# An earlier table of cache products, the first attention block inside the last projection chunk, and a split order for the output projection

## The chip, the cores and the metric

The kernel runs on one core of a Trainium2 chip. The metric is device time in microseconds (us) for one launch. The engines are named as in the profile: PE (matrix multiplies and transposes), PEld (its weight loads), DVE (vector), ACT (scalar, activations), POOL (GpSimd), SP (here it only issues DMAs). Every engine works through its own instructions strictly in the order of its program and waits on semaphores of the others.

## The reference

One inference step of a two-layer trunk for 512 prompt tokens and 8 x 8 sample tokens, all in float32. Layer 0 mixes by dilated attention, layer 1 by a diagonal state-space layer; each is followed by a gated feed-forward layer. The change touches layer 0's attention alone:

```python
DIL_GROUPS = ((128, 1), (512, 4), (2048, 16)); HEAD_DIM = 64; N_HEAD_SLOTS = 8
qkv = (h @ w_qkv).reshape(B, T, 3, N_DIL, N_HEAD_SLOTS, HEAD_DIM)
q = rope(rmsnorm(qkv[:, :, 0], q_gain), pos)
k = rope(rmsnorm(qkv[:, :, 1], k_gain), pos)
v = qkv[:, :, 2]
...      # per group: keys = cache + new, scores * 64**-0.5, keys at 0, d, 2d, ..., window
p = jnp.exp(s - lse[..., None])
o = jnp.einsum('bqhk,bqkhd->bqhd', p, vf)
wts = jax.nn.softmax(jnp.stack(lses, axis=0), axis=0)
return jnp.einsum('gbqh,gbqhd->bqhd', wts, jnp.stack(outs, axis=0)) @ w_o
```

The prompt has no cache. Each of the 8 sample rows (b = 0..7, 8 tokens each) attends to its own cache of 128, 512 and 2048 positions; a query uses 129 keys of each group.

## The kernel before

**The projection** (`qkv_phase`) makes q, k and v for three groups in nine chunks of 512 columns, in the order of `CHUNKS`. A chunk has four steps, so there are 36 steps, j = 0..35. A step takes 256 rows of `w_qkv`: each weight tile is split into a rounded high part `whi` (ACT) and a remainder `wlo` (DVE), and PE multiplies four tiles of 128 prompt tokens (`xh`, `xl`) and one of the sample tokens (`xsp`) into five PSUM tiles `acc`. At a chunk's end ACT and DVE evict the five tiles (`a`); for q and k DVE then does norm and rotation over the next steps (`finish`: three instructions for each tile, table `TURNS`), and PE transposes the results. v of group 1 is the last chunk.

**Cache work woven into the steps.** After each `acc` tile of a step comes a slot (`slot`), in which PE gets a little of other work, five slots to a step. Three kinds of it bear on this case:

- *Units of keys* (`SCORES`, class `Score`): for a sample row b and group 1 or 0, PE transposes cached keys (`pt<-ident,kc`), ACT evicts them (`ks<-pt`), and PE multiplies them with the row's queries into a PSUM tile `Sd` (`Sd<-ks,Q..`). DVE then masks `Sd` into `Sall` and takes a maximum (`Sall<-Sd,md`, `mx`).
- *Pairs* (`PAIRS`): for group 2, SP loads a tile of cached keys and the row's queries from DRAM (`kc<-cache_kv_w`, `kc<-qscr`, 512 KB each), and DVE multiplies them and sums over a head (`kc<-kc`, `P<-kc`). The pairs of step j are loaded in step j-1 and queued on DVE at the start of step j, behind the step's `wlo` and `finish` work. A row has four pairs.
- *Close* (`Close2`): ten slots after a row's fourth pair was queued, or later if a unit is half done, PE transposes the row's sums into `Sd` (`Sd<-ident,P`, `Sd<-kT,Q`), and DVE masks them like a unit's.

There is one `Sd` buffer: the next user's matmuls wait until DVE has read the last one's. The orders of PE, DVE, ACT and SP here are kept as written (`kept`, `keep_in_program_order`).

**Attention** (`attn_phase`) runs 16 blocks n (four head pairs by four token residues): score matmuls `S` (`scores`), mask and maximum on DVE (`masked`: `sm<-S,mp`), exponential on ACT (`exps`), transposes of the probabilities (`turn`: `pt<-ident,sm`), and products with v (`values`: `O`). Beside them the eight sample rows are worked (`Decode`): softmax of the row's scores `Sall` (maximum `dnm`, exponential, reciprocal, scale), transposes into `Sd`, products with cached values (`Sd<-kc,Pz`, 27 MB of values come in by SP), the row's own v (`vn`, by way of DRAM, `vscr`), and the copy into `att`.

**The output projection** (`wo_phase`) splits `att` into `ath` (ACT) and `atl` (DVE), splits four weight tiles of `w_o` as above, and multiplies.

Of the kernel before, what the change touches and what calls it, by code (L numbers as in the profile page):

```python
# [18 lines left out]
D = 1024  # L19
# [4 lines left out]
KT = 8  # L24
# [27 lines left out]
def _build(nc, tc, A, es):  # L52
# [71 lines left out]
    with ExitStack() as qs:  # L124
        atp = right("atp")
        at_ = atp.__enter__()
        att = at_.tile([128, 4, NT], F32, name="att")
        rs_ = ExitStack()
        dsp = rs_.enter_context(right("dsp"))
        Sall = dsp.tile([128, NB, 3, 136], F32, name="Sall")  # L130
        mx3 = dsp.tile([128, NB, 3], F32, name="mx3")
        md = dsp.tile([128, 3, 136], BF16, name="md")
        kst = rs_.enter_context(right("kst", bufs=KST))
        qk = qs.enter_context(pool("qk"))
        qT = [att] + [qk.tile([128, 4, NT], F32, name=f"qT{i}") for i in (1, 2)]
        kT = [qk.tile([128, 4, NT], F32, name=f"kT{i}") for i in range(3)]
        vscr = scr.tile([3, 64, 512], F32, name="vscr")
        qscr = scr.tile([64, 512], F32, name="qscr")
        vtscr = scr.tile([4, 128, 512], F32, name="vtscr")
        xscr = scr.tile([128, KT, NT], F32, name="x_scr")  # L140
        with ExitStack() as p1:
            acc = p1.enter_context(tc.tile_pool(name="acc", bufs=5, space=PSUM))
            c1 = p1.enter_context(pool("c1"))
            vt, mp = qkv_phase(nc, tc, A, p1, locals())
        with ExitStack() as p2:
            attn_phase(nc, tc, A, p2, locals())
        rs_.close()
# [184 lines left out]

def qkv_chunk(nc, L, x, begin, step, pre=None, slot=None):
    acc = L["acc"]
# [6 lines left out]
    for kk in range(4):  # L341
        wh, wl = begin()
        for t in range(4):
            if pre is not None:
                pre(kk, t)
            for k2 in range(2):
                k = kk * 2 + k2
                ah, al = x.h[:, k, t * 128:(t + 1) * 128], x.l[:, k, t * 128:(t + 1) * 128]
# [5 lines left out]
        for k2 in range(2):  # L354
            k = kk * 2 + k2
            mm(ps[4], x.s[:, k, :], wh[:, k2, :], start=k == 0, stop=False)
            mm(ps[4], x.s[:, k, :], wl[:, k2, :], start=False, stop=k == KT - 1)
        if slot is not None:
            slot()
        step()  # L360
# [54 lines left out]
def qkv_phase(nc, tc, A, es, L):  # L415
# [77 lines left out]
    def begin():  # L493
# [6 lines left out]
        for gi in SCORES.get(j, ()):  # L500
            b, n = fill[gi].pop(0), UNITS[gi]
            cached.append((gi, b, [cache_tile(nc, A, kst, "kc", gi, b, c0, min(2, n - c0), 0, kept) for c0 in range(0, n, 2)]))
        due = [ready.pop(0) for _ in range(PAIRS.get(j, 0))]
# [138 lines left out]

    def v_chunk(gi, wk, vt=None):
        ps = qkv_chunk(nc, L, x, begin, step, None, slot)
        for t in range(5):
            if t == 4:
# [8 lines left out]
            kv_out(nc, A, gi, 1, t, a)  # L655

    for part, gi in CHUNKS[:8]:
# [10 lines left out]

    def values():
        nc.sync.dma_start(vt0, L["vtscr"].rearrange("t p c -> p t c"))  # L670
        nc.sync.dma_start(mp, A["c_mp"])

    notes[34] = values
# [5 lines left out]
    return [vt0, vt1, vt2], mp  # L679

# [10 lines left out]
def attn_phase(nc, tc, A, es, L):  # L691
# [19 lines left out]

    den, rd, S2, PT, sm, P0, P12, O = {}, {}, {}, {}, {}, {}, {}, {}

    def scores(n):
# [3 lines left out]
        S2[n] = [pS.tile([128, 512], F32, name="S") for _ in range(2)]  # L718
        for b in range(4):
            for h in range(2):  # L720
                o, k = S2[n][h][b * 32:b * 32 + 32, 0:256], kT[0][half[h], hp, max(b - 1, 0) * 128:(b + 1) * 128]
                if not b:
                    o, k = o.rearrange("p (a c) -> p a c", a=2), k[:, None, :].to_broadcast([64, 2, 128])
                mm(o, qT[0][half[h], hp, r * 128 + b * 32:r * 128 + b * 32 + 32], k, start=True, stop=True, tile_position=(h * 64, b * 32))
        sl = slice(r * 128, r * 128 + 128)
        for gi in (1, 2):
            for h in range(2):
                mm(S2[n][h][:, (gi + 1) * 128:(gi + 2) * 128], qT[gi][half[h], hp, sl], kT[gi][half[h], hp, sl], start=True, stop=True)

# [6 lines left out]
    def exps(n, h):  # L736
        x, nm = sm[n][h]
        s.activation(x, x, AF.Exp, bias=nm, scale=-1.0, accum_out=den[n // 4][:, n % 4, h:h + 1])

# [21 lines left out]

    def values(n):
        hp, r = divmod(n, 4)
# [9 lines left out]
        for b in range(4):  # L773
            for pv in (1, 0):
                if b == 0 and pv == 0:
                    continue
                for j in range(4):
                    mm(o_[j * 32:j * 32 + 32, :, b, :], vt[0][:, b - 1 + pv, hp * 128 + j * 32:hp * 128 + j * 32 + 32], P0[hp][j // 2][:, pv, b],
                       start=False, stop=True, tile_position=(0, j * 32))
        R = pS.tile([128, 512], F32, name="S")  # L780
        for c in range(4):
# [9 lines left out]
    class Decode:  # L791
        def __init__(self, b):
            self.b, self.u = b, 0
            P = Sall[:, b].rearrange("p a b -> p (a b)")
            nm, dn, rd = (dk.tile([128, 1], F32, name=x, bufs=2) for x in ("dnm", "ddn", "drd"))
            v.tensor_reduce(nm, mx3[:, b, :], AX.X, OP.max)
            v.tensor_scalar(nm, nm, -SCALE, None, op0=OP.mult)
            s.activation(P, P, AF.Exp, bias=nm, scale=SCALE, accum_out=dn)
            v.reciprocal(rd, dn)
            v.tensor_scalar(P, P, rd, None, op0=OP.mult)  # L800
            self.pw = dk.tile([128, 24], F32, name="pw")
            v.tensor_copy(self.pw.rearrange("p (a b) -> p a b", a=3), Sall[:, b, :, 128:136])
            self.vn = dk.tile([24, 512], F32, name="vn", bufs=2)
# [46 lines left out]

    dec = {}
    for n in range(20):
        if n < 16:
            scores(n)
        if 1 <= n < 17:
            turn(n - 1)
        if n < 16:
            masked(n)
        for h in range(2):
            if 1 <= n < 17:  # L860
                evict(n - 1, h)
            if n < 16:
                exps(n, h)
        if n % 2 and n // 2 < 8:
            dec[n // 2].turn()
        if n % 2 == 0 and 0 <= n // 2 - 2 < 8:
            dec[n // 2 - 2].out()
        if 2 <= n < 18:
            values(n - 2)
            dec[n // 2 - 1].values(n % 2)  # L870
        if n % 2 == 0 and n < 16:
            dec[n // 2] = Decode(n // 2)


def wo_phase(nc, tc, A, es, L):
    v, s, g, te = nc.vector, nc.scalar, nc.gpsimd, nc.tensor
    pool, xT, att, load_w, mm6, acc, n0 = (L[x] for x in ("pool", "xT", "att", "load_w", "mm6", "acc", "n0"))
# [4 lines left out]
    atl = wk.tile([128, 4, NT], F32R, name="atl")  # L882
    for k in range(4):
        s.activation(ath[:, k], att[:, k], AF.Copy)
        v.tensor_tensor(atl[:, k], att[:, k], ath[:, k].bitcast(F32), OP.subtract)
    for c in range(4):
        wh, wl = load_w(A["w_o"], D, 0, 4, c * 256, 256, 0.0)
        for m in range(2):
            ps = acc()
            for k in range(4):  # L890
                mm6(ps, wh[:, k, m * 128:(m + 1) * 128], wl[:, k, m * 128:(m + 1) * 128], ath[:, k], atl[:, k], k == 0, k == 3)
            f = 2 * c + m
            xv = xr[:, f, :T].rearrange("p (r i) -> p i r", r=4)
            for h, i0, i1 in ((0, 0, 72), (1, 72, 128)):
                v.tensor_tensor(xT[:, f, 4 * i0:4 * i1].rearrange("p (i r) -> p i r", r=4), ps[:, h, :4 * (i1 - i0)].rearrange("p (i r) -> p i r", r=4), xv[:, i0:i1], OP.add)
            v.tensor_tensor(xT[:, f, T:], ps[:, 1, T - HN:HN], xr[:, f, T:], OP.add)
            n0.add(2 * c + m)
# [598 lines left out]
```

## Time and profile before

| | us |
|---|---|
| three runs | 1518.72, 1525.94, 1526.87 (median 1525.94) |
| the profiled execution | 1525.21 |
| its span | 1523.4 |
| PE busy | 1480.0 (97%) |
| projection, to the first `S` matmul | 0 to 319.5 |
| attention, to the first matmul with `ath` | 319.5 to 419.5 |

Spans and starts are in us from the start of the span. A row of the timeline gives start, duration, engine, line, operation, output<-input, shapes, the count, and in brackets how long the engine had been idle before it and what ended that. A row of the waits gives who waited for whom, the total, the number of times and the longest. PEclk in a row by windows is the granted PE clock, 1.00 being full speed.

### The profile page before, as it was taken

The page shows a single profiled execution, that of the slowest core. Times are in us where ns is not written, and L with a number is a line of the kernel's source. Part 1 is how long each engine was busy: PE and PEld are TensorE (multiplying, and loading weights), DVE is VectorE, ACT ScalarE, POOL GpSimd, SP SyncE. Part 2 cuts the span into 40 slices and gives each one's busy share as a digit, 9 for nine tenths or more (in the row PEclk, how much of TensorE's full clock was granted, in tenths as well). Part 3 has the DMA queues.
Part 4 walks back from the last instruction along what each step waited for, and adds up shares of the span by engine and source line. Part 5 has one row for each costly group of instructions (what it writes and reads, how often), then busy time and mean ns, then how long its engine had stood idle before and what let it go on. Part 6 is the DMA issues. An engine that isn't in the chain of part 4 may idle for free. (4 is left out here: it accounts for less than half of the span.)

```text
span 1523.4 us, 29540 instructions
## 1 busy us (share of the span) xinstructions
PE 1480.0 (97%) x12406; PEld 1388.4 (91%) x12406; DVE 910.8 (60%) x1507; ACT 520.9 (34%) x790; POOL 315.2 (21%) x369
## 2 busy tenths in 40 slices
PE   9999999789999999999999999999999999999998
PEld 7877777557799999999999999899999999999998
DVE  5899988545467853688887568754443333333332
ACT  4523445345553221222123363432332212221222
POOL 2021132310031019544434330020110001000100
PEclk9999999979999999999999999999999999999999
DMA  7568587979775555797666828865546555442222
GB/s 253 190 242 299 187 288 236 345 261 311 256 231 191 194 199 195 243 302 257 240 242 238 301 97 252 267 206 191 190 164 221 190 191 192 149 151 89 83 63 76
DMA packets 190460, 322.62 MB, mean 212 GB/s; under 512 B 39480, under 2 KB 137016, under 8 KB 188792
## 3 DMA queue, kind: packets, MB, share of 16 engines
q1 hardware_dynamic: 182808, 303.63, 58.3%
q10 hardware_dynamic: 4992, 10.04, 1.9%
q0 software_dynamic: 2528, 7.08, 1.3%
q8 instruction: 97, 1.59, 0.4%
q14 instruction: 35, 0.29, 0.1%
HBM read 289.22 MB, written 118.78 MB: 268 GB/s over the span
## 5 line engine op out<-in xcount | busy, mean ns | idle before, releaser
L107 PE MATMUL acc<-xgl,whi 128*128 128x288 f32 x1760 | 378.6, 296 | 1.0 <-DVE xgl L172 1.0
L107 PE MATMUL acc<-xgh,wlo 128*128 128x288 f32 x1760 | 377.7, 296 | 0.0
L107 PE MATMUL acc<-xgh,whi 128*128 128x288 f32 x1760 | 377.1, 296 | 0.1
L101 DVE TENSOR_TENSOR wlo<-raw,whi 128x1024 fp32r<-128x1024 f32 (+1 forms) x168 | 207.6, 1236 | 238.1 <-ACT whi L100 234.8
L100 ACT ACTIVATE whi<-raw 128x1024 fp32r<-128x1024 f32 (+1 forms) x168 | 174.5, 1039 | 458.6 <-PE acc L107 404.8
L107 PEld LDWEIGHTS acc<-xgl,whi 128*128 128x128 f32 x1760 | 282.6, 188 | 2.5 <-DVE xgl L172 1.3
L107 PEld LDWEIGHTS acc<-xgh,wlo 128*128 128x128 f32 x1760 | 282.7, 188 | 0.6 <-issue 0.2
L107 PEld LDWEIGHTS acc<-xgh,whi 128*128 128x128 f32 x1760 | 281.8, 188 | 0.5 <-DVE gt L933 0.3
L935 POOL TENSOR_TENSOR gt<-gt,rstd 128x576 f32<-128x576 f32 x44 | 77.1, 1754 | 431.1 <-ACT gt L934 431.0
L107 PE MATMUL acc<-hh,whi 128*128 128x288 f32 x704 | 151.4, 296 | 0.0
L107 PE MATMUL acc<-hh,wlo 128*128 128x288 f32 x704 | 151.2, 295 | 0.0
L107 PE MATMUL acc<-hl,whi 128*128 128x288 f32 x704 | 151.0, 295 | 0.0
L337 PE MATMUL acc<-whi,xh 128*128 128x512 f32 x288 | 119.7, 417 | 1.2 <-ACT a L688 0.7
L107 PEld LDWEIGHTS acc<-hh,wlo 128*128 128x128 f32 x704 | 113.2, 188 | 0.2 <-issue 0.2
L107 PEld LDWEIGHTS acc<-hl,whi 128*128 128x128 f32 x704 | 113.0, 188 | 0.2 <-issue 0.2
L337 PE MATMUL acc<-wlo,xh 128*128 128x512 f32 x288 | 113.1, 394 | 0.0
L107 PEld LDWEIGHTS acc<-hh,whi 128*128 128x128 f32 x704 | 113.1, 188 | 0.0
L337 PE MATMUL acc<-whi,xl 128*128 128x512 f32 x288 | 112.3, 395 | 0.0
L192 POOL TENSOR_TENSOR ssum<-ssum,sq 128x576 f32<-128x576 f32 x21 | 36.2, 1723 | 232.4 <-ACT sq L191 232.4
L337 PEld LDWEIGHTS acc<-whi,xh 128*128 128x128 f32 x288 | 54.6, 190 | 12.3 <-ACT a L688 1.7
L337 PEld LDWEIGHTS acc<-whi,xl 128*128 128x128 f32 x288 | 54.6, 190 | 12.1
L947 DVE TENSOR_TENSOR xT<-acc,xT 128x576 f32<-128x576 f32 x48 | 36.2, 754 | 48.1 <-PE acc L107 48.1
(362 smaller groups left out, 2015.9 us busy)
## 6 DMA issues: line engine op xcount, KB each, us to landing
o_kv_s<-cache_kv_w SPq DMA_DIRECT2D x64, 1020.0 KB, 7.5
kc<-cache_kv_w SPq DMA_DIRECT2D x96, 512.0 KB, 6.7
raw<-ffn_w_gate SPq DMA_DIRECT2D x44, 512.0 KB, 3.6
raw<-ffn_w_up SPq DMA_DIRECT2D x44, 512.0 KB, 3.6
raw<-ffn_w_down SPq DMA_DIRECT2D x40, 512.0 KB, 3.4
raw<-w_qkv SPq DMA_DIRECT2D x36, 512.0 KB, 6.5
kc<-qscr SPq DMA_DIRECT2D x32, 512.0 KB, 6.1
o_kv_s<-cache_kv_w SPq DMA_DIRECT2D x16, 1008.0 KB, 6.1
```

The lines of the kernel that those rows point to most:

```text
L100: s.activation(hi, raw, AF.Copy)
L101: mark[0] = v.tensor_tensor(lo, raw, hi.bitcast(F32), OP.subtract)
L107: te.matmul(ps[:, c, :HN], w, x[:, c * HN:(c + 1) * HN], start=first and i == 0, stop=last and i == 2)
L192: g.tensor_tensor(self.ss, self.ss, sq, OP.add)
L337: ins = nc.tensor.matmul(*a, **kw)
L935: g.tensor_tensor(t, t, nin.r, OP.mult)
L947: v.tensor_tensor(xv, ps[m][:, :, :HN], xv, OP.add)
```

## The change

1. `PAIRS`: one pair more in step 20 and in step 24, one fewer in steps 33 and 34. So rows 3 to 6 get their fourth pair 1 to 2 steps earlier, and their Close with it.
2. `SCORES`: group 1 has no unit in step 24, and its last six move on by one step (25 to 30); the eight units of group 0 come two at a time in steps 31 to 34, loaded by one 512 KB DMA into one buffer (before, two of 256 KB in two).
3. The last chunk (steps 32 to 35) works each step in the order samples, tiles 0 to 3, and in step 35 evicts each tile as it ends. Behind the sample tile, row 0's softmax is queued (`row_soft`); behind tile 0, the scores of attention block 0 (`score_block`, into the two `pt` buffers, with the masked result in two key buffers); behind tile 2, their exponentials. The attention loop starts with block 1.
4. At the end, row 7's last products come ahead of block 15's, and its output between block 15's products and its scaling.
5. `wo_phase`: the splits of the first two `w_o` tiles are queued behind the exponentials of block 6 (before: ACT 300.45 and 318.63 in the profile), and for the first of them all products with `ath` come ahead of those with `atl`. Two `ffn_w_gate` loads and a cache shift, `o_kv_s` (2 MB together), which SP issued from 303 on, move into the middle of the attention.
6. The loads of the mask `mp` and of `vt0` keep their place on SP in steps 34 and 35 (before, both in 34).

```diff
-PAIRS = {..., 19: 1, 21: 1, 22: 1, 23: 1, 24: 1, 25: 1, ..., 31: 1, 32: 2, 33: 2, 34: 2}
-SCORES = {22: (1,), 23: (1,), 24: (1,), ..., 29: (1,), 30: (0,), 31: (0, 0), 32: (0, 0), 33: (0, 0), 34: (0,)}
+PAIRS = {..., 19: 1, 20: 1, 21: 1, 22: 1, 23: 1, 24: 2, 25: 1, ..., 31: 1, 32: 2, 33: 1, 34: 1}
+SCORES = {22: (1,), 23: (1,), 25: (1,), ..., 30: (1,), 31: (0,), 32: (0,), 33: (0,), 34: (0,)}
...
+    notes[34] = lambda: kept(nc.sync.dma_start(mp, A["c_mp"]))
+    notes[35] = lambda: kept(nc.sync.dma_start(vt0, L["vtscr"].rearrange("t p c -> p t c")))
+    def then(t):
+        if t == 4:
+            row_soft(v, s, Sall, mx3, 0, *soft)
+        if t == 0:
+            S0.extend(ptp.tile([128, 4, 128], F32, name="pt").rearrange("p a b -> p (a b)") for _ in range(2))
+            score_block(lambda *a, **kw: kept(te.matmul(*a, skip_group_check=True, **kw)), S0, qT, kT, 0)
+            sm0.extend((kst.tile([128, 2, 512], F32, name="kc")[:, 0, :], f) for f in (f0, f1))
+            for h in range(2):
+                v.tensor_tensor_reduce(sm0[h][0], S0[h], mp[:, 0, :], -SCALE, 3e38, OP.add, OP.min, sm0[h][1])
+        if t == 2:
+            for h in range(2):
+                s.activation(sm0[h][0], sm0[h][0], AF.Exp, bias=sm0[h][1], scale=-1.0, accum_out=den0[:, 0, h:h + 1])
     with ExitStack() as e4:
-        v_chunk(1, e4.enter_context(pool("wk2")), vt1)
+        v_chunk(1, e4.enter_context(pool("wk2")), vt1, (4, 0, 1, 2, 3), then)
...
+def row_soft(v, s, Sall, mx3, b, nm, dn, rd, pw):
+    P = Sall[:, b].rearrange("p a b -> p (a b)")
+    v.tensor_reduce(nm, mx3[:, b, :], AX.X, OP.max)
+    v.tensor_scalar(nm, nm, -SCALE, None, op0=OP.mult)
+    s.activation(P, P, AF.Exp, bias=nm, scale=SCALE, accum_out=dn)
+    v.reciprocal(rd, dn)
+    v.tensor_scalar(P, P, rd, None, op0=OP.mult)
+    v.tensor_copy(pw.rearrange("p (a b) -> p a b", a=3), Sall[:, b, :, 128:136])
...
+    dec[7].values(1)
+    values(15, dec[7].out)
+    return mark[6]
...
     for c in range(4):
-        wh, wl = load_w(A["w_o"], D, 0, 4, c * 256, 256, 0.0)
+        raw = fetch_w(A["w_o"], D, 0, 4, c * 256, 256, 0.0)
+        if c < 2:
+            with tc.issue_after(L["amark"].ins):
+                wh, wl = split_w(raw)
+        else:
+            wh, wl = split_w(raw)
+        ps = [acc() for _ in range(2)]
+        if c == 0:
+            for ws, x in (((wh, wl), ath), ((wh,), atl)):
+                ...
```

Two places show what this does to the engines' orders.

**DVE, the end of step 29**, before. The rows are the step's pair and the mask of the unit that PE finishes at the step's end:

```order
L688 TENSOR_TENSOR a_2286<-a_2286,rq_2298 128x512
L688 TENSOR_TENSOR kc_2312<-kc_2312,kc_2314 128x1024
L688 TENSOR_REDUCE P2_2059<-kc_2312 128x2x4x2
L688 ISA Sall_76,mx3_77<-Sd_2498,md_78 128x136
L688 ISA mx3_77 128x1
L688 TENSOR_TENSOR wlo_2561<-raw_2429,whi_2560 128x1024
```

and now:

```order
L742 TENSOR_TENSOR a_2247<-a_2247,rq_2259 128x512
L742 TENSOR_TENSOR kc_2273<-kc_2273,kc_2275 128x1024
L742 TENSOR_REDUCE P2_2281<-kc_2273 128x2x4x2
L742 ISA Sall_76,mx3_77<-Sd_2431,md_78 128x136
L742 ISA mx3_77 128x1
L742 ISA Sall_76,mx3_77<-Sd_2464,md_78 128x136
```

Row 5's Close (`Sd_2431`) has moved from step 31 into the first slot of step 29; its mask stands behind the whole of the step's DVE work. The unit `Sd_2464`, whose first matmuls stand on PE after the step's third tile, uses the same PSUM buffer and so waits for that mask.

On PE the Close now stands between the step's first two tiles, in the first slot:

```order
L339 MATMUL acc_2262<-whi_2277,xl_127 128x512
L409 MATMUL Sd_2431<-ident_63,P2_1823 128x128
L412 MATMUL Sd_2431<-kT2_96,Q2_2145 32x8 x4
L559 MATMUL pt_2438<-ident_63,kc_2269 128x128 x4
L339 MATMUL acc_2263<-whi_2277,xh_126 128x512
```

Before, the same stretch of PE held only the transposes `pt<-ident,kc` between the two tiles.

**ACT, step 35**, before:

```order
L688 ACTIVATE ks_3059<-pt_3054 128x512
L100 ACTIVATE whi_5029<-raw_5027 128x1024
L688 ACTIVATE ks_3112<-pt_3107 128x512
L688 ACTIVATE vt1_2806<-acc_2811,rr_335 128x512
L688 ACTIVATE vt1_2806<-acc_2812,rr_335 128x512
```

and now:

```order
L742 ACTIVATE ks_3034<-pt_3029 128x512
L742 ACTIVATE ks_3082<-acc_2813,rr_342 64x512
L742 ACT_TABLE_LOAD
L742 ACTIVATE Sall_76,f3_83<-Sall_76,f2_82 128x408
L742 ACTIVATE ks_3104<-pt_3099 128x512
L742 ACTIVATE vt1_2804<-acc_2809,rr_342 128x512
L742 ACTIVATE ks_3137<-pt_3132 128x512
```

The eviction of the step's first transposed keys (`ks_3104<-pt_3099`) now stands behind the sample tile's eviction, a table load and row 0's exponential. On PE, the second half of block 0's scores (`pt_3109`) takes the buffer that this eviction frees.

More of the change, by code (lines that the diff above doesn't have):

```diff
@@ L132, in _build @@
         md = dsp.tile([128, 3, 136], BF16, name="md")
+        den0 = dsp.tile([128, 4, 2], F32, name="den")
+        first = [dsp.tile([128, n], F32, name=f"f{i}") for i, n in enumerate((1, 1, 1, 1, 1, 24))]
         kst = rs_.enter_context(right("kst", bufs=KST))
@@ L330, in prep, with qkv_chunk @@
                 self.roots()
-def qkv_chunk(nc, L, x, begin, step, pre=None, slot=None):
+def qkv_chunk(nc, L, x, begin, step, pre=None, slot=None, order=range(5), ends=None):
     acc = L["acc"]
@@ L342, in qkv_chunk @@
         wh, wl = begin()
-        for t in range(4):
+        for t in order:
             if pre is not None:
@@ L353, in qkv_chunk @@
                 slot()
[L354 to L359, printed above, removed]
+            if ends is not None and kk == 3:
+                ends(ps, t)
         step()
@@ L641, in qk_chunk, with v_chunk, ends @@
             works.setdefault(turn[0] + i, []).append(lambda t=t, ahead=4 if (gi, part, t) == (0, 1, 3) else ahead: finish(t, ahead))
-    def v_chunk(gi, wk, vt=None):
-        ps = qkv_chunk(nc, L, x, begin, step, None, slot)
-        for t in range(5):
+    def v_chunk(gi, wk, vt=None, order=range(5), then=None):
+        def ends(ps, t):
             if t == 4:
@@ L655, in v_chunk @@
             kv_out(nc, A, gi, 1, t, a)
+            if then is not None:
+                then(t)
+        if then is None:
+            ps = qkv_chunk(nc, L, x, begin, step, None, slot)
+            for t in range(5):
+                ends(ps, t)
+        else:
+            qkv_chunk(nc, L, x, begin, step, None, slot, order, ends)
     for part, gi in CHUNKS[:8]:
@@ L678, in qkv_phase, with score_block @@
     assert not any(fill) and not ready and not raws and not splits
-    return [vt0, vt1, vt2], mp
+    return [vt0, vt1, vt2], mp, (sm0, den0, soft[3])
+def score_block(mm, S, qT, kT, n):
+    half = [slice(0, 64), slice(64, 128)]
+    hp, r = divmod(n, 4)
+    for b in range(4):
+        for h in range(2):
+            o, k = S[h][b * 32:b * 32 + 32, 0:256], kT[0][half[h], hp, max(b - 1, 0) * 128:(b + 1) * 128]
+            if not b:
+                o, k = o.rearrange("p (a c) -> p a c", a=2), k[:, None, :].to_broadcast([64, 2, 128])
+            mm(o, qT[0][half[h], hp, r * 128 + b * 32:r * 128 + b * 32 + 32], k, start=True, stop=True, tile_position=(h * 64, b * 32))
+    sl = slice(r * 128, r * 128 + 128)
+    for gi in (1, 2):
+        for h in range(2):
+            mm(S[h][:, (gi + 1) * 128:(gi + 2) * 128], qT[gi][half[h], hp, sl], kT[gi][half[h], hp, sl], start=True, stop=True)
+def row_soft(v, s, Sall, mx3, b, nm, dn, rd, pw):
[6 more added lines that the diff above has]
+    v.tensor_copy(pw.rearrange("p (a b) -> p a b", a=3), Sall[:, b, :, 128:136])
 class Kept:
@@ L710, in mm @@
         return te.matmul(*a, skip_group_check=True, **kw)
-    den, rd, S2, PT, sm, P0, P12, O = {}, {}, {}, {}, {}, {}, {}, {}
+    rd, S2, PT, P0, P12, O, mark = {}, {}, {}, {}, {}, {}, {}
+    sm, den = {0: L["head"][0]}, {0: L["head"][1]}
     def scores(n):
@@ L718, in scores @@
         S2[n] = [pS.tile([128, 512], F32, name="S") for _ in range(2)]
[L719 to L728, printed above, removed]
+        score_block(mm, S2[n], qT, kT, n)
     def masked(n):
@@ L760, in evict, with values @@
             v.reciprocal(rd[hp], den[hp])
-    def values(n):
+    def values(n, between=lambda: None):
         hp, r = divmod(n, 4)
@@ L779, in values @@
                        start=False, stop=True, tile_position=(0, j * 32))
+        between()
         R = pS.tile([128, 512], F32, name="S")
@@ L793, in __init__ @@
             self.b, self.u = b, 0
[L794 to L802, printed above, removed]
+            if b:
+                self.pw = dk.tile([128, 24], F32, name="pw")
+                row_soft(v, s, Sall, mx3, b, *(dk.tile([128, 1], F32, name=x, bufs=2) for x in ("dnm", "ddn", "drd")), self.pw)
+            else:
+                self.pw = L["head"][2]
             self.vn = dk.tile([24, 512], F32, name="vn", bufs=2)
@@ L849, in out @@
                 v.tensor_copy(att[half[h], :, q0:q0 + 8], ot[half[h], :, h * 8:h * 8 + 8])
-    dec = {}
-    for n in range(20):
-        if n < 16:
+    dec = {0: Decode(0)}
+    for n in range(18):
+        if 0 < n < 16:
             scores(n)
@@ L856, in attn_phase @@
             turn(n - 1)
[L857 removed]
+        if 0 < n < 16:
             masked(n)
```

63 lines of the change are left out of this document (39 added, 24 removed).

## The prediction

> **What bounds the kernel now.** I read the page's totals first, then PE's waits from 156 us on, then the timeline at the longest of them, then windows at the places where the granted clock is low.
>
> ```profile
> span 1523.4 us, 29540 instructions
> ...
> PE 1480.0 (97%) x12406; PEld 1388.4 (91%) x12406; DVE 910.8 (60%) x1507; ACT 520.9 (34%) x790; POOL 315.2 (21%) x369
> ```
>
> PE is the bound: it idles 43.4 us of the span. The change takes no matmul away, so it can win only PE's idle time and the time that PE runs at half clock. PE's waits in the later steps, from 156 to 312 us (total, times, longest):
>
> ```profile
> PE Sd L563 <- DVE mx L688: 10.4, 5, 7.4
> PE Sd L407 <- DVE mx L688: 1.4, 1, 1.4
> ```
>
> at the attention's start, 319 to 336 us:
>
> ```profile
> PE S L688 <- DVE nm L688: 1.1, 1, 1.1
> PE pt L688 <- ACT sm L688: 0.9, 1, 0.9
> PE Sd L688 <- DMA vn<-vscr: 0.8, 1, 0.8
> ```
>
> and around its end, 412 to 424 us:
>
> ```profile
> PE acc L107 <- ACT ath L884: 1.2, 1, 1.2
> PE Sd L688 <- ACT os L688: 0.5, 1, 0.5
> ```
>
> The longest is at the end of step 34: PE waits for DVE's mask, DVE for its pairs, and the pairs for a DMA.
>
> ```profile
> 301.25 1.22 DVE L688 TENSOR_TENSOR kc<-kc 128x1024 f32<-128x1024 f32 x1 [7.84 <-DMA kc<-qscr]
> ...
> 307.63 0.29 DVE L688 CUSTOM_DVE_ANT_0 Sall<-Sd,md 128x136 f32<-128x136 f32 x1
> ...
> 308.07 0.66 PE L563 MATMUL Sd<-ks,Qy 128*32 128x128 f32 x8 [7.44 <-DVE mx L688]
> ```
>
> After each of three groups of waits the clock is halved for a while:
>
> ```profile
> 308.00:313.80 5.80, 5.72 (x28) 4.68 (x29) 0.31 (x2) 0.00 (x0) 0.00 (x0) 0.50 0.84 303
> 324.10:330.90 6.80, 6.21 (x41) 4.37 (x42) 3.33 (x15) 4.58 (x15) 1.67 (x2) 0.50 0.19 68
> 419.60:423.00 3.40, 3.40 (x15) 3.40 (x16) 2.60 (x4) 1.53 (x3) 0.00 (x0) 0.51 0.79 314
> ```
>
> Half of PE's busy time there is lost: 2.9, 3.1 and 1.7 us. The stretches are multiples of about 3.4 us.
>
> **What the change can win.** Steps 33 and 34 lose a pair each, and group 0's keys come in half as many DMAs. The wait of 7.4 and its 2.9 at half clock should go; so should the 1.4, and of the five waits on `mx` all but one that stays:
>
> ```profile
> 280.41 0.42 PE L563 MATMUL Sd<-ks,Qy 128*32 128x128 f32 x8 [1.54 <-DVE mx L688]
> ```
>
> Step 32 keeps its two pairs. So 10.4 + 1.4 - 1.5 + 2.9 = 13.2 us. At the start of the attention block 0's chain (mask, table load, exponentials) now lies under matmuls, and `vn` can leave nearly a step earlier, as the sample tile now comes first: 1.1 + 0.9 + 0.8, and 3.1 at half clock, 5.9 us. At the end 1.2 + 0.5 and 1.7, 3.4 us. In all 22.5 us, if nothing new comes in.
>
> **What it costs, step 20.** DVE has no idle time here:
>
> ```profile
> 156.50 1.22 DVE L688 TENSOR_REDUCE P<-kc 128x16 f32<-128x1024 f32 x1
> ...
> 167.81 0.68 DVE L688 TENSOR_TENSOR a<-a,rq 64x512 f32<-64x512 f32 x1
> ...
> 168.76 0.46 PE L629 MATMUL pt<-ident,a 64*128 64x64 f32 x4
> ```
>
> The added pair costs two such instructions, 2.45 us. PE's transposes at 168.76 follow DVE's last rotation (end 168.49) by 0.27, so PE takes nearly all of it: 2.2 us. Bounds: 0, if DVE's idle moments cover it, and 2.5. I take 2.2, since DVE works without a pause up to the transposes. The second pair of step 24 meets pauses of DVE:
>
> ```profile
> 197.26 0.69 DVE L688 TENSOR_REDUCE sh<-t 128x8 f32<-128x512 f32 x1 [1.14 <-ACT t L688]
> ```
>
> The other 1.3 of its 2.45 makes DVE late for tiles that PE transposes a step later, and for masks; I take no cost, with bounds of 0 and 1.3. The unit that step 25 loses on PE is made in step 30, so it cancels.
>
> **Step 29** is the largest cost. Its rows before:
>
> ```profile
> 245.18 0.65 PE L563 MATMUL Sd<-ks,Qz 128*32 128x128 f32 x16
> ...
> 248.83 1.22 DVE L688 TENSOR_TENSOR kc<-kc 128x1024 f32<-128x1024 f32 x1
> 250.08 1.22 DVE L688 TENSOR_REDUCE P<-kc 128x16 f32<-128x1024 f32 x1
> 251.22 0.29 DVE L688 CUSTOM_DVE_ANT_0 Sall<-Sd,md 128x136 f32<-128x136 f32 x1
> ```
>
> and DVE in the window from 240.5 to 251.2 (length, then busy time of PE, PEld, DVE):
>
> ```profile
> 240.50:251.20 10.70, 10.70 (x89) 8.21 (x87) 10.39 (x18) 4.41 (x7) 3.29 (x9) 1.00 0.70 229
> ```
>
> The unit's first matmuls start at 245.18 without a wait, and DVE has no pause up to 251.22. Now Close 5 sits in the first slot of this step, and its mask stands where the mask at 251.22 stood, behind the split, the norm, two rotations and the pair. The unit's first matmuls need that mask. The Close itself puts them 0.5 later, at 245.7; they can start 0.45 after the mask's start (as 307.63 to 308.07 in step 34), at 251.7. Both move with the step, so the difference stays: 6.0 us. Behind them on PE stand the rest of the step and all further steps; nothing hides it. Bounds: 0, if DVE is ahead by so much (a gain is excluded, a wait starts nothing earlier), and 7, if the step comes 1 us earlier on PE and not on DVE; step 24's late pair could do that. An idle time of this length is followed by half clock; the nearest row is the 7.44, after which 5.8 us ran at half. I take 2.6 us of loss (a little under its 2.9; bounds 1.7, one stretch, and 3.4, two). Together 8.6.
>
> **Step 32.** Close 6 stands between the last two units' matmuls, each behind the other's mask: one more wait of 0.6 us, as DVE's mask and its read take 0.45 after PE's end.
>
> **Step 35.** A chain of old durations in a new order:
>
> ```profile
> 314.63 0.60 ACT L688 ACTIVATE ks<-pt 128x512 f32<-128x512 f32 x1 [13.12 <-PE pt L551]
> ...
> 319.71 0.69 ACT L688 ACTIVATE ks<-acc,rr 64x512 f32<-64x512 f32 x1
> ...
> 322.50 1.28 ACT L688 ACT_TABLE_LOAD   x1 [2.11 <-DVE nm L688]
> ...
> 325.23 0.62 ACT L688 ACTIVATE Sall<-Sall,dnm 128x408 f32<-128x408 f32 x1
> ```
>
> From the sample tile's end ACT needs 0.69 (eviction), 1.28 (table), 0.62 and some 0.2 (exponential and the read of its sum; DVE's part runs under the table load) and 0.60 (eviction of the keys): 3.5 us with the gaps. PE has one tile (1.4) and four transposes (0.5) in that time: it waits 1.6 us. Bounds: 0.5, and 2.6 if the load waits for DVE as it did at 322.50; I take 1.6, as the order puts no wait on it. One more `Sd` hand-over at the step's end adds 0.5, block 1's exponentials 0.3. As for the clock, at 324.1 it fell after little more than 1 us of waiting, so I expect another stretch here, 1.7, and at even odds one more at block 1, 0.9. In all 5.0, with bounds of 1.3 and 7.
>
> The Trainium skill, "TensorE: Matmul & The Clock Gate", section "HAM oscillation", puts the limit at gaps of over some 3.4 us, with a window of that length that runs freely. By that rule step 29 is still followed by a slow stretch, step 35 and block 1 by none, and the result would be 2.6 us lower, 1518, inside the main case's range. The stretches here have the page's length, but the drops at 324.1 and 419.6 followed gaps of at most 1.2 us: there this trace speaks against the rule.
>
> **The rest.** Each weight split inside the attention is as wide as the 1.22 us product above and stands on ACT and on DVE ahead of a block's work: 0.5 us for both, between 0 and 2.4. The 2 MB that move there have room on the queues between loads. At the end block 15's output is evicted on ACT, then scaled on DVE:
>
> ```profile
> 414.87 1.15 ACT L688 ACTIVATE att<-O 128x512 f32<-128x512 f32 x1 [3.60 <-PE O L688]
> ```
>
> `ath` of the first three head pairs needs no scaling of block 15's, but stands on ACT behind the eviction: 1.15 and some 0.7 of its own after O's end, 1.9 with a gap, while PE has about 1.1 to 1.3 of transposes and sums left. I take 0.8 of waiting. With a fair chance of half clock after it (0.5): 1.3.
>
> **The sum.** 22.5 - 2.2 - 8.6 - 0.6 - 5.0 - 0.5 - 1.3 = 4.3 us won. The profiled execution took 1525.2, so 1520.9; that execution lies 0.7 under the median of the runs shown, inside their spread, and I forecast 1521 us.
>
> **The rivals.** *No new wait in step 29* (chance 0.27). Against it: DVE's rows from 241 to 251 are back to back. For it: if DVE reaches step 29 some 6 us ahead of PE, the mask is ready in time. Then 8.6 more is won: 1512.
>
> *The DMA's hole stays* (0.13): the result is slower than before. Place: the pair of step 33. Its queries (`kc<-qscr`) take a buffer that the first pair of step 32 frees. Before, this step had a wait already:
>
> ```profile
> 285.06 1.23 DVE L688 TENSOR_TENSOR kc<-kc 128x1024 f32<-128x1024 f32 x1 [2.65 <-DMA kc<-qscr]
> ```
>
> From the first pair's end, some 8 us into step 32, to DVE's want in step 33 are 5 us; PE's second unit of step 33 tolerates a landing of up to 8.5. Beyond that point it is PE that waits, then the next step's loads start later too. If the loads of `w_o` and values fill the queues as they did up to 308, the 7.4 and the 2.9 stay: 1520.9 + 10.3 = 1531. Against it: two pairs fewer, 1 MB each, and no `ffn_w_gate` in that stretch.
>
> *Nothing is won at the attention's start* (0.10): the half clock only moves into block 1 and 2, 5.9 less 1.0 is lost: 1526, no change.
>
> **How the numbers follow.** The main case has 0.50, with a range of its own of 1516 to 1526: 5 us to either side, about what step 29's clock, step 35 and step 24 leave open together. About 0.5%, 7.6 us, is what a measurement can tell here, so faster means under 1518.3, slower over 1533.6. Faster: 0.25 of the first rival, 0.12 of the main case: 0.37. Slower: 0.06 of the second and 0.02 of the main case: 0.08. The rest, 0.55, is no change. The range, 1509 to 1528, takes in the first rival with a little more, and leaves out most of the second.
>
> **What would show it.** In the changed kernel's profile: a wait of PE at `Sd<-ks,Qz` in step 29, near 246 us, of 5 to 7 us on `mx`, with a half clock behind it; no wait over 2 us from step 33 on; PE waiting 1 to 2 us on ACT inside block 0's score matmuls near 310; no `vn` wait; under 1 us ahead of `ath`. I'm wrong if step 29 has no such wait, or if the wait on `qscr` is still there.

## The result, and the profile after

The changed kernel is slower: 1532.17 us, median of 16 runs (1527.11 to 1538.38), beside 1524.35 for 16 runs of the kernel before (1518.72 to 1528.39). The ratio is 1.0052, with a 95% interval of 1.0040 to 1.0064. The forecast was 1521, within 0.5% of the kernel before, and a range up to 1528: it was wrong in size and in sign.

The profiled execution took 1534.21 us. The page's totals of the changed kernel:

```profile
span 1532.4 us, 29536 instructions
...
PE 1481.5 (97%) x12406; PEld 1389.3 (91%) x12406; DVE 913.9 (60%) x1507; ACT 520.0 (34%) x790; POOL 316.1 (21%) x369
```

PE idles 50.9 us of the span; before it was 43.4. PE's busy time grew by 1.5 us with the same 12406 matmuls, which is more time at half clock. So 7.5 of the span's 9.0 us are waits. PE's waits from 150 to 450 us (total, times, longest):

```profile
PE Sd L571 <- DVE mx L742: 6.5, 2, 6.0
PE pt L637 <- DVE a L742: 4.1, 3, 1.7
PE acc L947 <- DVE cwd L1174: 3.3, 1, 3.3
PE Sd L571 <- ACT ks L742: 2.6, 1, 2.6
PE Sd L742 <- DVE Sall L742: 2.2, 1, 2.2
...
PE Sd L742 <- DMA kc<-cache_kv_w: 1.6, 2, 0.9
```

The waits that the change was credited with are gone: the 7.4 of step 34, step 33's 1.4, the `nm`, `sm` and `vn` waits at the attention's start. New ones stand in their place. The one forecast for step 20 is 1.66 (the 1.7 of the second row) and is read further down. The next is the wait forecast for step 29, seen on the timelines of DVE and PE:

```profile
243.79 1.26 DVE L742 TENSOR_TENSOR wlo<-raw,whi 128x1024 fp32r<-128x1024 f32 x1
...
253.84 0.29 DVE L742 CUSTOM_DVE_ANT_0 Sall<-Sd,md 128x136 f32<-128x136 f32 x1
...
254.28 1.08 PE L571 MATMUL Sd<-ks,Qz 128*32 128x128 f32 x16 [5.99 <-DVE mx L742]
```

Between the first two rows DVE works without a pause: split, norm, two rotations, pair, and only then Close 5's mask, for which PE waits.

Another was costed at nothing. In step 24 the second pair stands on DVE ahead of the sums of squares (`sh<-t`), on which ACT waits, and PE waits for ACT:

```profile
199.16 1.22 DVE L742 TENSOR_TENSOR kc<-kc 128x1024 f32<-128x1024 f32 x1 [1.47 <-DMA kc<-qscr]
...
201.62 2.06 DVE L742 TENSOR_REDUCE sh<-t 128x8 f32<-128x512 f32 x3
...
202.33 0.63 ACT L742 ACTIVATE t<-a 128x512 f32<-128x512 f32 x1 [3.89 <-DVE sh L742]
202.87 0.58 ACT L742 ACTIVATE ks<-pt 128x512 f32<-128x512 f32 x1
...
203.50 0.43 PE L571 MATMUL Sd<-ks,Qz 128*32 128x128 f32 x8 [2.64 <-ACT ks L742]
```

The pair's queries came 1.47 us late from the DMA, and DVE stood still for them. Meanwhile ACT had its next square to write, `t`, whose buffer is free only after DVE's sum. ACT stood 3.89 us, and behind that square in its queue was the eviction of the transposed keys, which PE needed.

A third lies at the splits of `w_o`, now inside the attention:

```profile
357.52 2.00 ACT L100 ACTIVATE whi<-raw 128x1024 fp32r<-128x1024 f32 x2
...
358.60 2.36 DVE L101 TENSOR_TENSOR wlo<-raw,whi 128x1024 fp32r<-128x1024 f32 x2 [1.46 <-ACT whi L100]
...
361.07 0.43 DVE L742 TENSOR_SCALAR Sall<-Sall,drd 128x408 f32<-128x408 f32 x1
...
361.65 0.52 PE L742 MATMUL Sd<-ident,Sall 128*128 128x128 f32 x3 [2.15 <-DVE Sall L742]
```

Both splits stand between the two halves of row 3's softmax, on both engines: ACT's two delay the exponential, DVE's two the scaling.

A fourth is at the end of the attention:

```profile
424.25 0.21 DVE L1113 COPY raw<-ldt 32x128 f32<-32x128 f32 x1 [7.80 <-DMA cw<-ssm_c_re]
424.48 0.39 DVE L742 COPY att<-Sd 64x32 f32<-64x32 f32 x2
424.90 1.10 DVE L742 TENSOR_TENSOR att<-att,S 128x512 f32<-128x512 f32 x1
425.89 0.24 DVE L1174 COPY cwd<-cw 128x128 f32<-128x128 f32 x1
...
425.03 1.26 ACT L742 ACTIVATE ath<-att 128x576 fp32r<-128x576 f32 x2 [2.21 <-DVE att L742]
...
426.15 0.51 PE L947 MATMUL acc<-ath,whi 128*128 128x288 f32 x2 [3.25 <-DVE cwd L1174]
```

A copy of 0.21 us for the state-space part, `raw<-ldt`, stands on DVE ahead of row 7's copies into `att` (in the kernel before it stood behind `atl`, at 427.64), and it waits for small loads that SP issued at 421 to 422. DVE idles 7.8 us, then `att`, `ath` and PE follow. The page names `cwd` as PE's releaser. The rows show the longer chain: `ath` began only at 425.03, behind `att`.

A fifth is small: the first two reads of cached values, 0.76 and 0.87 us (the 1.6 in the waits view). Other waits in the attention have no releaser in the profile ("issue"); they come to 3.2 us before and to 3.3 now.

A sixth lies behind this window, at the end of the output projection, where PE needs POOL's last sum of squares:

```profile
462.01 1.24 PE L199 MATMUL aux<-ssum,ones 128*128 128x288 f32 x4 [1.61 <-POOL ssum L194]
```

The kernel before has no wait there, and neither has the run below with the tables alone; all other runs have one, of 0.7 to 2.1 us. So it comes with the rest of the change. Which part makes it was not tried.

Windows where the clock was low, and one (312 to 330) where it wasn't, in the same form as in the prediction:

```profile
253.40:260.20 6.80, 5.92 (x32) 4.78 (x33) 0.74 (x3) 0.88 (x2) 0.00 (x0) 0.51 0.76 234
294.40:297.60 3.20, 3.20 (x22) 2.70 (x23) 2.48 (x4) 0.00 (x0) 2.90 (x6) 0.50 1.06 386
312.00:330.00 18.00, 15.89 (x178) 11.07 (x178) 5.93 (x23) 9.21 (x20) 6.88 (x13) 1.00 0.52 168
362.70:365.90 3.20, 3.20 (x68) 3.15 (x64) 1.33 (x9) 2.20 (x8) 0.00 (x0) 0.50 0.99 330
427.40:430.80 3.40, 3.40 (x17) 3.40 (x16) 1.40 (x3) 0.04 (x1) 0.00 (x0) 0.51 0.97 401
994.00:997.80 3.80, 3.80 (x21) 3.80 (x20) 3.77 (x8) 0.76 (x2) 1.15 (x2) 0.56 0.43 100
```

The loss at half clock is some 9.5 us, against 7.7 before; of it 1.7 lies at 994 us, in a part that the change doesn't touch.

### The profile page after: what moved, and what is told of

It is laid out like the page before. It is cut to its first block, busy times and chain, and to the rows that moved or that the text cites. A ratio compares the mean times of both kernels' runs of the same rounds, so it can differ in the third digit from the quotient of the medians.

```text
span 1532.4 us, 29536 instructions
## 1 busy us (share of the span) xinstructions
PE 1481.5 (97%) x12406; PEld 1389.3 (91%) x12406; DVE 913.9 (60%) x1507; ACT 520.0 (34%) x790; POOL 316.1 (21%) x369
## 4 chain that ended last, share of the span: by engine, by line
PE 51%; DVE 3%; DMA 3%; issue 1%; ACT 0%; DVEq 0%; ACTq 0%
PE acc L107 49%; DMA y_scr<-ys 1%; DMA u_scr<-uP 1%; PE aux L107 1%; DVE cb L1251 1%; DVE kk L1260 1%; DMA raw<-ffn_w_down 0%; PE aux L1244 0%; PE aux L1255 0%; DVE Z L1361 0%; PE aux L1017 0%; DMA U<-u_scr 0%; DVE wlo L101 0%; PE aux L1379 0%; PE aux L1380 0%
```

## The experiments

All times are medians. The kernel before took 1524.4 to 1524.9 us on the same chips. Ratios are to it. The changed kernel's 1.0052 comes from other runs. The single mends have intervals of about 0.15% (2.4 us) to either side, so a mend of 1 or 2 us isn't told from nothing by its time alone; there the trace says whether the wait went, and the time of all mends together whether it paid.

**Close 5 two steps later.** It stands in step 31, as before the change, and everything else stays.

```diff
-                later(10, lambda c=c: close(c))
+                later(20 if b == 5 else 10, lambda c=c: close(c))
```

> Row 5's Close is put back into step 31, 20 slots after its last pair and not 10; nothing else differs from the changed kernel. Theory A (each new stall adds its whole price to the end): PE's wait of 5.99 us in step 29 and the half clock from 253.4 to 260.2 behind it (about 3 us lost) go, no other wait takes their place: 9 us less, 1523 us against 1532 for the changed kernel, and step 31 has no wait on the mask, as in the kernel before. Theory B (DVE is the bound of these steps, and PE's wait only shows its lateness): the wait comes back in steps 30 to 32 at the rotated tiles or at the next masks, and the time falls by 3 us or less, to 1529 or more.

Measured 1526.28 us, ratio 1.0005 (0.9992 to 1.0019). DVE and PE in step 29 of this kernel:

```profile
253.56 0.29 DVE L742 CUSTOM_DVE_ANT_0 Sall<-Sd,md 128x136 f32<-128x136 f32 x1
...
247.53 0.64 PE L571 MATMUL Sd<-ks,Qz 128*32 128x128 f32 x16
```

DVE is where it was (253.56, was 253.84), but PE's row at 247.53, the unit's first matmuls, has no wait: it no longer needs that mask. In steps 30 and 31 no wait on a mask over 0.34 comes back. This one place costs 6 to 7 us (5.9 by the medians, 7.2 by the ratios), the wait of 5.99 with part of its half clock; theory A's 9 had counted all of that.

**The state-space copy behind `att`.** `raw<-ldt` is queued behind the last `atl`.

```diff
-            v.tensor_copy(raw[:, 2]...
+            with tc.issue_after(L["atm"].ins):
+                v.tensor_copy(raw[:, 2]...
```

> On DVE the copy of the state-space step sizes (it waits for a small load) is queued behind the last remainder of att; before, it stood ahead of the copies into att. Theory A (this copy blocks DVE in order, so att, ath and PE wait for the load): PE's wait ahead of the first product with ath falls from 3.25 us to about 0.8, the figure of the prediction, DVE's wait of 7.8 us moves behind the remainders, 2.4 us less, or 4 if the half clock behind it goes too: 1528 to 1530 us. Theory B (att is late through its own chain, the eviction of block 15's output and its scaling): the wait stays at 2 us or more, 1531 to 1532.

Measured 1530.94 us, ratio 1.0038 (1.0022 to 1.0055). PE in this kernel, and DVE's row behind the second of its waits:

```profile
418.55 0.50 PE L947 MATMUL acc<-ath,whi 128*128 128x288 f32 x2 [1.39 <-ACT ath L742]
...
429.37 0.49 PE L107 MATMUL acc<-ath,whi 128*128 128x288 f32 x2 [1.00 <-DVE xT L957]
...
428.00 1.09 DVE L956 TENSOR_TENSOR xT<-acc,xr 128x288 f32<-128x288 f32 x2 [5.39 <-DMA xr<-x_scr]
```

The wait at the first product fell from 3.25 to 1.39, and no half clock follows it. So the blocked copy was the cause of more than half of that wait. Of the 1.86 won, 1.00 comes back as a wait on the residual sums `xT`. Ahead of these sums DVE stood idle for the load of the residual `xr` (third row), not for the moved copy, which had ended at 422.6.

**The two splits apart**, behind the exponentials of blocks 7 and 9, no longer both behind block 6's.

```diff
-    return mark[6]
+    return mark[7], mark[9]
...
-            with tc.issue_after(L["amark"].ins):
+            with tc.issue_after(L["amark"][c].ins):
```

> The two splits of w_o inside the attention are queued behind the exponentials of blocks 7 and 9, one at a time, and not both behind block 6. Theory A (the pair of splits stood ahead of the softmax of a sample row on ACT and DVE, whose transposes PE takes next in block 7): the wait of 2.15 us at 361.65 and the half clock from 362.7 to 366 (1.7 us lost) go, and there is under 0.5 us at either new place: about 3.5 us less, 1528 to 1529 us. Theory B (any split inside the attention costs PE its length): two waits of about 1 us, no half clock, 1530 to 1531.

Measured 1532.92 us, ratio 1.0047 (1.0029 to 1.0065): not to be told from the changed kernel. The wait of 2.15 and its half clock are gone, but PE later has these:

```profile
387.42 1.94 PE L742 MATMUL Sd<-kc,Pz 128*32 128x128 f32 x59 [1.94 <-issue]
394.25 1.07 PE L742 MATMUL Sd<-kc,Pz 128*32 128x128 f32 x30 [1.05 <-issue]
```

They stand at the reads of cached values, and the profile names no releaser ("issue"). The changed kernel had such waits too, 1.41 at 371.74 and 1.09 at 412.47. All of this kind come to 3.3 us there and to 4.4 here, so about 1 us has moved. Where the rest of the gain went is not shown by the waits: this execution also has 3.3 us of loss at half clock behind steps 20 and 24, which the changed kernel's hasn't.

**Both splits late**, behind the exponentials of blocks 13 and 15.

```diff
-    return mark[6]
+    return mark[13], mark[15]
```

> The two splits of w_o are queued behind the exponentials of blocks 13 and 15; so the 2 MB of ffn_w_gate and the cache shift, which wait for the buffers that the splits free, are loaded after the last cached values. Theory A (these 2 MB make the cached values late from the middle of the attention on, whatever block the splits stand in): the wait of 2.15 us and its half clock go, and PE's waits for cached values after block 6 (1.4 and 1.1 in the changed kernel, 4.4 in all with the splits behind blocks 7 and 9) fall under 1 us together: 4 to 6 us less, 1526 to 1528 us. Theory B (the values are late because of the loads' pace alone): waits of 2 to 4 us for values stay, 1529 to 1531.

Measured 1531.49 us, ratio 1.0040 (1.0021 to 1.0059). Again the 2.15 is gone (0.61 is left at row 6), a wait of 1.95 without a releaser stands at 416.92, and the time isn't told from the changed kernel's. Waits without a releaser come to 2.9 us after block 6, so theory A, by which they should fall under 1 us, is out.

**The second pair of step 24 four slots later**, behind the sums of squares.

```diff
+            if j == 24 and i == 1:
+                later(4, lambda x=x: pair(*x))
+            else:
+                pair(*x)
```

> The second pair of step 24 is queued on DVE four slots later, behind the sums of squares and not ahead of them. Theory A (the pair held up the sums, these held the two buffers of squares, and ACT, in order, held up the evictions of keys behind a square): PE's wait of 2.6 to 3.4 us on ACT near 203 us goes, and with it a half clock that some executions show there: 2.6 to 5 us less, 1527 to 1530 us. Theory B (DVE is simply full until 225 us): a wait of the same size comes back at the masks or rotated tiles of steps 24 to 27, 1531 to 1532.

Measured 1530.67 us, ratio 1.0042 (1.0026 to 1.0057). PE in steps 24 and 25:

```profile
209.68 0.46 PE L643 MATMUL pt<-ident,a 64*128 64x64 f32 x4 [0.66 <-DVE a L748]
...
214.97 0.64 PE L577 MATMUL Sd<-ks,Qz 128*32 128x128 f32 x16 [0.59 <-DVE mx L748]
```

The 2.64 is gone, and 0.66 and 0.59 have come in, together 1.25, inside the bounds that the prediction had for the pair (0 to 1.3). So the place of the pair ahead of the sums made the wait; the pair itself costs PE 1.25.

**Three mends together**: Close 5 in step 31, the copy behind `att`, the splits apart.

> The three edits together: row 5's Close in step 31, the step-size copy behind att's remainders, the two splits behind blocks 7 and 9. Theory A (prices add): 9 + 2.4 to 4 + 3.5, about 15 to 16 us less than the changed kernel, 1516 to 1517 us, 7 to 8 us below the kernel before. Theory B (waits replace each other; time won in the projection is taken by the loads of cached values in the attention): half of it or less, 1524 or more, no faster than the kernel before.

Measured 1522.09 us, ratio 0.9990 (0.9976 to 1.0003), between the theories. By the ratios the three edits alone gave 0.47, 0.14 and 0.05%, 0.66% in sum, and together they give 0.62%: within the intervals they add, and theory A's prices for them were too high.

**The tables of before.** `PAIRS`, `SCORES` and the loads of group 0's keys are as before the change; the early row 0 and block 0, the splits and the end stay changed.

```diff
-PAIRS = {... 20: 1, ... 24: 2, ... 32: 2, 33: 1, 34: 1}
+PAIRS = {... 24: 1, ... 32: 2, 33: 2, 34: 2}
```

> The changed kernel with the old tables of pairs and units (and group 0's keys in two loads again); the last chunk's order, block 0 in step 35, the splits and the end stay as changed. Theory A (the tables' new waits in steps 20, 24 and 29 cost about as much as the hole of step 34 that they remove): the waits at 172, 203 and 254 us (1.7, 2.6, 6.0) and their half clock go, a wait of 5 us or more on the mask behind late queries comes back in step 33 or 34: 1529 to 1533 us. Theory B (the hole of step 34 came from the loads of ffn_w_gate and from keys in small loads next to it, which the rest of the change moves away anyway): no such hole, 1522 us or less.

Measured 1524.86 us, ratio 1.0001 (0.9989 to 1.0013), between the theories. Next to the other parts the tables cost 7 to 8 us (7.3 by the medians, 7.8 by the ratios). The hole that they should fill is here much smaller than before the change:

```profile
298.63 1.23 DVE L736 TENSOR_TENSOR kc<-kc 128x1024 f32<-128x1024 f32 x1 [4.97 <-DMA kc<-qscr]
...
304.21 0.43 PE L565 MATMUL Sd<-ks,Qy 128*32 128x128 f32 x8 [3.00 <-DVE mx L736]
```

and in the kernel before, DVE at the same place had a row more:

```profile
302.39 1.22 DVE L101 TENSOR_TENSOR wlo<-raw,whi 128x1024 fp32r<-128x1024 f32 x1
```

The queries are late by 4.97 instead of 7.84, and the split of `w_o` that stood between the pair's two instructions has moved into the attention: 2.87 + 1.2 = 4.1 of the 4.4 by which PE's wait is shorter. The other parts of the change had filled more than half of the hole by themselves.

**The tables alone, on the kernel before**: its `PAIRS` and `SCORES` and its loads of group 0's keys are those of the change, and nothing else.

> The kernel before with one part of the change only: the two tables of steps and the group 0 keys in loads of two blocks. Theory 'the tables only shift waits': they bring the 6.0 of step 29, the 2.6 of step 24 and some 1.4 at step 20, and take away what the kernel before still has in steps 33 and 34, the hole of 7.4 with its half clock (2.9), 1.5 of shorter mask waits and the 1.4; so here, where the hole is whole, they come out near nothing: 1522 to 1527. Rival 'the tables cost 7 us whatever stands beside them', as they did against the changed kernel with the old tables: 1531 to 1533.

Measured 1529.12 us, ratio 1.0033 (1.0017 to 1.0048), between the two theories. PE's waits, 150 to 450 us:

```profile
PE Sd L569 <- DVE mx L694: 7.0, 3, 6.0
...
PE Sd L569 <- ACT ks L694: 2.7, 1, 2.7
```

The hole of 7.4 is gone here without the rest of the change, and the 6.0 and the 2.7 are in. My near-zero balance set 10.0 us of new waits against 13.2 won, and the 13.2 alone had half clock in it. In the profiled execution PE idles 4.1 us more than before (47.5, was 43.4), and it is busy 1.9 us longer (1481.9, was 1480.0), which is more time at half clock. So the tables lose even with the whole hole to win (4 to 5 us), and lose more (7 to 8) beside parts that fill it too. The difference, about 3 us, fits the 4.4 that the old-tables run showed; the intervals don't settle it to the microsecond.

**Five mends**: Close 5 in step 31; both splits late; step 24's second pair four slots later; `raw<-ldt` and `cwd` queued behind the first residual sums, not behind `atl`; and one pair moved from step 32 to step 31.

```diff
-         32: 2, 33: 1, 34: 1}
+         31: 2, 32: 1, 33: 1, 34: 1}
...
+            if c < 2:
+                am = last
...
-                    v.tensor_copy(cwd, ...
+                    with tc.issue_after(L["atm"].ins):
+                        v.tensor_copy(cwd, ...
```

> Five edits of the changed kernel: Close 5 in step 31; the step-size copies behind the first residual sums; the splits behind blocks 13 and 15; step 24's second pair four slots later; one of step 32's two pairs in step 31. Theory A (prices add): from 1532, 7 for step 29 (as measured alone), 2 to 3 for the end, 4 for the splits and values, 3 for step 24, 2 to 3.5 for step 32 and its half clock: 1512 to 1515 us, 9 to 12 below the kernel before. Theory B (each mend uncovers the next wait): 1518 to 1522.

Measured 1520.11 us, ratio 0.9976 (0.9961 to 0.9991), in the range of theory B. The moved pair made a new wait in step 31, this time straight on DVE's mask:

```profile
270.63 0.70 PE L577 MATMUL Sd<-ks,Qz 128*32 128x128 f32 x16 [3.66 <-DVE mx L748]
```

**Four mends**: the same without the moved pair.

> The five mends without the moved pair: step 31 has one pair and step 32 two, as in the changed kernel; Close 5 in step 31, the copies at the end behind the first residual sums, both splits late and step 24's second pair four slots later stay. Theory 'the moved pair made the wait of 3.66 in step 31': that wait and its half clock go, 1.5 to 2.0 in step 32 come back, 1517 to 1519.5. Rival 'VectorE is late by that pair anywhere': a wait of over 3 us appears in step 32 in its place, 1520 to 1522.

Measured 1517.63 us, ratio 0.9955 (0.9942 to 0.9968): 0.45% faster than the kernel before. PE's largest waits, 150 to 450 us:

```profile
PE pt L643 <- DVE a L748: 3.5, 3, 1.7
PE Sd L748 <- DMA kc<-cache_kv_w: 1.7, 2, 1.0
PE Sd L409 <- DVE mx L748: 1.5, 1, 1.5
```

No wait over 1.7 us is left there. The 3.66 is gone, and step 32's 1.48 is back beside its 0.52, so the moved pair had made the wait.

**The tables of before with the mends of the end and the splits.**

> The changed kernel with the tables and loads of before, the two copies at the end behind the first residual sums, and the splits behind the exponentials of blocks 13 and 15. Theory 'the tables are the whole loss and the rest of the change is a gain that the end and the splits eat': against the same kernel without the two mends (1524.9) 3 to 4.5 us are won, 1520 to 1522. Rival 'the waits at the end and at the splits only move': 1524 to 1526.

Measured 1518.21 us, ratio 0.9960 (0.9947 to 0.9973). The hole's 3.0 stays; the end's wait is 1.38 instead of 3.7. Both this and the four mends beat both kernels, and the two are not told apart. They differ by the tables, with Close 5 and step 24's second pair in their mended places. So with these two places mended the tables cost nothing that was measured here, and they win nothing either.

## Why the prediction was wrong

The profiled execution (1534.21, 2.0 over the median) is 13.3 us over the sum of 1520.9. Its terms, as the traces have them:

| step of the prediction | forecast | the profile after |
|---|---|---|
| steps 33 and 34, won | 13.2 | the waits and the half clock are gone |
| step 20 | 2.2 | 1.66, and 0.7 more at 181 us |
| step 24 | 0 | 2.64 |
| step 29, wait | 6.0 | 5.99 |
| step 29, clock | 2.6 | 3.0 |
| step 32 | 0.6 on top of 1.5 | 1.47 and 0.52, and 1.6 at half clock |
| step 35 and block 1, waits | 2.4 | 1.14 + 0.52 = 1.7 |
| step 35 and block 1, clock | 2.6 | 0 |
| splits | 0.5 | 2.15, and 1.6 at half clock |
| cached values | not in the sum | 0.76 + 0.87 |
| the end | 0.8, and 0.5 for the clock | 3.25, and 1.7 at half clock |
| POOL's sum at 462 us | not in the sum | 1.61 |
| half clock at 994 us | not in the sum | 1.7 |

Step 20 is read from two rows of each trace, PE's transposes in the step ahead and in it; this is the kernel before,

```profile
155.47 0.63 PE L629 MATMUL pt<-ident,a 128*128 128x128 f32 x4 [1.20 <-DVE a L688]
```

and this the changed one:

```profile
156.87 0.63 PE L637 MATMUL pt<-ident,a 128*128 128x128 f32 x4 [1.18 <-DVE a L742]
...
172.39 0.46 PE L637 MATMUL pt<-ident,a 64*128 64x64 f32 x4 [1.66 <-DVE a L742]
```

From one to the other PE took 168.76 - 155.47 = 13.29 before and 172.39 - 156.87 = 15.52 now: 2.2 more. That this is the forecast's figure is chance. Only the 1.66 is waiting; most of the rest is PE's work for row 3's Close, which stood behind these rows before (174.76) and now stands between them (168.70). The first rows also differ, by 1.4 us, in a part where the change does nothing.

At step 35 PE waits inside block 0's scores for the eviction that stands behind row 0's exponential, as forecast, and then 0.52 at the `Sd` hand-over (325.49):

```profile
317.97 0.66 PE L695 MATMUL pt<-kT,att 64*32 64x256 f32 x14 [1.14 <-ACT ks L742]
```

The misses, with their sign: 1.4 ahead of step 20, -0.5 in it, 0.7 at 181 us, 2.6 in step 24, 0.4 for step 29's clock, 1.6 for step 32's, -0.7 and -2.6 for step 35's waits and clock, 3.3 at the splits, 1.6 for the values, 3.7 at the end, 1.6 at 462 us, 1.7 at 994 us. That is 14.8, of which 13.3 show; the rest is spread over small rows.

**Right:** the place, the mechanism and the size of the largest cost. Step 29's wait came within 0.01 us, and putting Close 5 back in step 31 took it away. It is 5.97 to 5.99 in all six profiled kernels that have Close 5 in step 29, with or without half clock ahead of it, so the figure is no luck: both engines move with the step, as the prediction had argued. The first rival, no wait in step 29, has fallen with it: DVE's rows stayed back to back. The second rival, the DMA's hole stays, has fallen too: no wait in steps 33 and 34. The third, nothing won at the attention's start, has fallen: the half clock at 324 us is gone and didn't move into blocks 1 and 2.

**Wrong, step 24** ("I take no cost, with bounds of 0 and 1.3"). The step counted DVE's time alone. It didn't ask who waits for the sums of squares that are queued behind the pair. It was ACT, whose queue holds the keys that PE needs, and the pair added a wait of its own for the DMA. In the run with the pair four slots later the 2.64 and that wait for the DMA go, and the 1.25 that stays lies in the bounds.

**Wrong, the end** ("I take 0.8 of waiting"). The step went through ACT's queue (`ath` behind the eviction) and not through DVE's. There the changed order has a copy that waits for loads ahead of the copies into `att`. With that copy moved, the wait is 1.39, near the 0.8 of the step, and it is on `ath`: the forecast's chain was the second longest.

**Wrong in size, the splits** (0.5; the wait of 2.15 lies under the upper bound of 2.4, the 3.75 with its half clock over it). The step spread them as work ahead of a block. They stand inside row 3's softmax on two engines, one after the other. That moving them pays was not shown by one run alone: in both single runs other waits took the place.

**Left out:** the cached values' 1.6 and the 1.61 on POOL's sum at 462 us. The sum had no term for either, and the cause of both stays open. That the values are wanted sooner because the start of the attention is quicker is argued, not shown; no run tried it.

**The clock** was over-forecast at step 35 and missed at step 32, the splits and the end. That the sums still lie near each other is luck: 3.0 + 1.6 + 1.6 + 1.7 = 7.9 against 2.6 + 2.6 + 0.5 = 5.7.

**The gain was credited to the wrong part.** The sum was for the whole change, so this moved no term of it. But the tables were taken as the gain (10.3 us in the hole with its clock), and the rest as extras. The runs show the reverse: the tables as made cost 4 to 8 us, with two places mended nothing that was measured, and the rest, with the end and the splits mended, makes the kernel 0.4% faster.

## What to carry to other kernels

When an instruction is moved ahead of others on an in-order engine, cost what stands behind it there and whose queue each of those feeds, not its own duration: a pair that costs PE 1.25 us in a better place cost 2.64 through ACT, and a copy of 0.21 us made more than half of a wait of 3.25. Before a part is credited with a wait that it removes, look whether another part of the same change shrinks that wait anyway. And when several new waits are found, mend them together: only Close 5's mend was told from nothing by its time alone (5.9 us), and with the other three it gave 14.5 us.

## What the runs showed of the hardware

The same wait costs a different amount at half clock, by where it falls. In the changed kernel PE stops at 248.3 in step 29, and up to 3.4 us later the clock is still full:

```profile
250.00:251.70 1.70, 0.00 (x0) 0.00 (x0) 1.63 (x4) 0.00 (x0) 0.00 (x0) 1.00 0.29 77
```

It falls at 253.3, and 5.92 us of work then run at half. In the run with the copy behind `att` the same wait of 5.98 begins at 247.15, and the clock falls some 2 us into it:

```profile
248.80:250.50 1.70, 0.00 (x0) 0.00 (x0) 1.63 (x4) 0.00 (x0) 0.00 (x0) 0.63 0.29 77
```

It is full again at about 256.1, 2.9 us after the work resumed: a loss of 1.5 instead of 3.0. Both stretches are 6.8 us long; the earlier one falls, the more of it lies in the wait. The one at step 34 of the kernel before began inside the wait too, at 303.6, and was 10.2 long.

At step 20 all ten profiled kernels with the new tables wait 1.66 us. In five of them the clock falls behind it, as in the run with Close 5 later (first row), and in five it doesn't, as in the run with the copy behind `att` (second row):

```profile
172.00:173.70 1.70, 1.70 (x6) 1.31 (x5) 1.67 (x3) 0.00 (x0) 0.32 (x1) 0.50 0.16 53
...
172.00:173.70 1.70, 1.70 (x9) 1.40 (x8) 1.63 (x3) 0.14 (x1) 0.08 (x1) 1.00 0.29 77
```

Where the clock falls there, it costs PE nothing. From the transposes at step 20 to those at 181.47 PE takes 9.08 us in the changed kernel, with the clock full and a wait of 1.25 at the end, and 9.08 in the run with Close 5 later, with the stretch at half and no wait (170.29 to 179.37). In both the transposes start 0.15 after DVE's last rotation has ended, so DVE sets their time.

By the length of the wait, the profiled kernels with the new tables show a fall as follows: 1.13 to 1.15 us (step 35) 0 of 9, 1.66 (step 20) 5 of 10, 2.5 to 3.4 (step 24) 5 of 7, 5.97 to 5.99 (step 29) 6 of 6. So a forecast for this kernel can give half clock a probability by the length of the wait, and not a size; one profiled execution is no more than one draw of it.

The Trainium skill, "TensorE: Matmul & The Clock Gate", section "The HAM clock gate (the "warmup" mystery)", describes a window of 3413 ns that runs freely, so that the moment of a change depends on where in it the work falls: the two step 29 rows agree. Its section "HAM oscillation", with the rule of gaps over some 3.4 us, agrees with step 35, where 1.14 us was followed by no drop; it doesn't agree with step 20, where 1.66 us was followed by one in half of the executions, nor with the 0.88 to 1.08 us ahead of the stretch at 324.1 in the kernel before.
